# VectorE's order in the down stage as one chain, with a third of the bank reads as ScalarE copies and accumulating DMAs

## The chip, the cores and the metric

The kernel runs on one core of a Trainium2 chip. Its engines are TensorE (matmuls and transposes; PE, its weight loads PEld), VectorE (DVE), ScalarE (ACT) and GpSimd (POOL); SyncE (SP) issues most of the DMAs, POOL the rest. Each engine has its own queue of instructions, taken in order. The metric is the device time of one execution in microseconds (us), as the median of several runs.

## What is computed

A two-layer encoder step on 1024 prompt tokens and 8 x 16 sample tokens: 1152 rows of 1024 features, nine tiles of 128 rows. Each layer is attention (sliding window with sinks in layer 0, chunked attention over a shared K/V in layer 1) and a squared-ReLU MLP. Only the second half of the MLP and its neighbours matter here:

```python
def mlp(x, g_norm, w_up, w_down):
    return jnp.square(jax.nn.relu(rmsnorm(x, g_norm) @ w_up)) @ w_down

for layer in range(DEPTH):          # DEPTH = 2
    ...                             # attention, residual added to hp and hs
    hp = hp + mlp(hp, g_mlp[layer], w_up[layer], w_down[layer])
    hs = hs + mlp(hs, g_mlp[layer], w_up[layer], w_down[layer])
```

Everything is float32. A float32 product is made of three matmuls on operands split into a high part (rounded, made by ScalarE as a cast) and a low part (the rest, made by VectorE as a subtraction): high x high, high x low, low x high. In the code that is `split` (lines 125 to 134) and `mm3` (line 744).

## The kernel before

The stages of a layer follow each other: `attention`, `wo_phase`, `mlp_up`, `mlp_down`. Instructions are written in the order of the program, and a scheduler then fixes each engine's order by a simulated timeline, with priorities and with added order edges (`behind`, line 750, puts one instruction behind another on its engine). The order on the chip is static.

**The up stage** (line 778) computes h = relu(x w_up)^2 in 16 blocks of 256 features. After each pair of blocks, `forms_even` and `forms_odd` (lines 917 and 929) build, with VectorE, sums and differences of h between token groups, and store 20 such forms to DRAM (`hd`, through POOL's queue, 192 KB a store).

**The down stage** (line 967) is h w_down plus the residual, by a fast matrix multiplication: 20 products (`RANK`) per half of the hidden features, two halves, so 40 products per layer. The nine token tiles are three parts of three (`PARTS`: part 0 is tiles 5, 6, 7; part 1 is 2, 3, 4; part 2 is the sample tile, 0 and 1), the columns two halves of 512, so there are six outputs `o`; `o // 2` is the part. One product takes a form of h (`a`, 128 x 1536 floats, one for all three tiles of a part) and a sum or difference of blocks of w_down (`w`, 128 x 2048), and multiplies in three blocks, one per tile: 3 x 4 x 3 = 36 matmuls of 512 columns into three PSUM banks. The products stand in chains (`CHAINS`): within a chain the banks go on accumulating, and after a product the banks may be read and added to, or subtracted from, outputs. The chains and signs give 41 reads per layer, each of three banks (line 1115: VectorE, 128x512, `x = x + or - bank`), so 123 instructions.

Around product n, in program order:
- `load_w(n + 3)` loads the blocks of w_down that are not there yet (tiles `r`, 1 MB each), `load_h` the next form (768 KB, tile `a`); `a` has three buffers, chosen by `slot`, but only two for the last six products (`TAIL`). All these loads and those of the residual tiles `x` run on SP's queue in one chain (`load`, line 1026).
- `split_w(n + 1)` makes the high and low part of w and of a for the next product: two ScalarE casts, two VectorE subtractions. w has two buffers.
- `add_w(n + 2)` sums two blocks of w_down on VectorE into `s` (two buffers); eight of the 40 products use one block alone and need no sum, and the last four sum in place in `r`.
- the matmuls of the three blocks, each followed by its reads.

All nine residual tiles `x` (512 KB each) are loaded early: parts 2 and 1 before product 0, part 0 around product 2 (`X_AT`, keyed by n + `AHEAD`). When a part has had its last read it is stored: to `xd` in DRAM for the next layer, or to the output.

`DOWN_HOME` (line 1773) lists the down stage's tiles in the order of their addresses; a tile can be loaded once the up stage's tile at the same address is no longer used. `RAW_AT` says which `r` buffer takes which block of w_down. The last `forms_odd` of the up stage is written at a lowered priority (`LATER`), so VectorE does its sums during the first products of the down stage.

Of the kernel before, what the change touches and what calls it, by code (L numbers as in the profile page):

```python
# [8 lines left out]
F32 = mybir.dt.float32  # L9
# [40 lines left out]
NEG_H = ((4, 6), (6, 12, 1))  # L50
RAW_AT = ((1, 3, 2, 7, 0, 6, 9, 8), (5, 3, 10, 6, 7, 8, 4, 9))
EPS = 1e-6
# [42 lines left out]
class Build:  # L95
# [682 lines left out]
    def mlp_up(self, layer, sx, x8, rp, raw0):  # L778
        nc = self.nc
        tt = nc.vector.tensor_tensor  # L780
        with ExitStack() as st:
# [114 lines left out]
            for b in range(NFB):  # L896
                quad, ws = weights(b)
                eh = [hp.tile([P, 3 * 3 * P], F32, tag="h", name="h", bufs=7) for _ in range(2)]
                if b == 0:
                    tokens(eh, quad, ws, slice(0, 256), False)  # L900
                    tokens(eh, quad, ws, slice(256, 512), True)
                else:
                    tokens(eh, quad, ws, slice(0, 512), True)
                if b % 2 == 0:
                    even = eh
                    self.forms_even(b // 2, eh)
                else:
                    with self.tc.high_priority(-LATER) if b == NFB - 1 else nullcontext():
                        self.forms_odd(b // 2, even + eh, hp.tile([P, 3 * 3 * P], F32, tag="h", name="ht", bufs=7))

# [18 lines left out]
    def forms_odd(self, c, eh, extra):  # L929
        tt, put = self.nc.vector.tensor_tensor, self.form_store(c)  # L930
        add, sub = ALU.add, ALU.subtract
        (a0, s10, a8), (a1, a5, s11), (a2, a6, a10), (a3, a7, a11) = map(self.form_cut, eh)
        u, w, z = self.form_cut(extra)
# [33 lines left out]
    def mlp_down(self, layer, out):  # L967
# [3 lines left out]
        with ExitStack() as st:  # L971
            self.psum_pools(st, f"dn{layer}", dict(z=(2, 1), c=(6, 1)), dict(c="c"))
            kinds = dict(
                a=([P, 2, 4, 3 * P], F32R), w=([P, 2, 4, 512], F32R), r=([P, 4, 512], F32),
                s=([P, 4, 512], F32), x=([P, D], F32),
            )
            homes, slots, xs = {}, {}, {}
# [8 lines left out]
            for n, tags in enumerate(DOWN_HOME):  # L986
                pool = self.pool(st, f"d{n}_{layer}")
                for t in tags.split():
# [5 lines left out]
                    else:  # L994
                        homes[t] = pool
                        slots[t] = fresh(t)
            for t in range(NTILE):
                xs[t] = slots.pop(f"x{t}")

            N = [slice(0, 512), slice(512, 1024)]  # L1000
# [22 lines left out]
            def slot(n):  # L1023
                return 1 + n % 2 if n >= total - TAIL else n % 3

# [21 lines left out]
            def add_w(n):  # L1047
# [13 lines left out]
                if g < 0:  # L1061
                    x, y = y, x
                tt(src[n], x, y, ALU.add if plus else ALU.subtract)  # L1063

            def split_w(n):
                if n >= total:
                    return
                w = ws[n] = take(f"w{n % 2}")
                self.split(w[:, 0], w[:, 1], src.pop(n))
                a = aa[n]  # L1070
                self.split(a[:, 0], a[:, 1], a[:, 1].bitcast(F32))

            banks = None

            def early(n):
                return self.tc.high_priority(EARLY[n]) if n < len(EARLY) else nullcontext()

            def load_x(i):
                for t in PARTS[i]:
                    load(xs[t], self.xd[t])  # L1080

            for n in range(AHEAD):
                with early(n):
                    load_w(n)
                    load_h(n)
                if n in X_AT:
                    load_x(X_AT[n])
            add_w(0)
            split_w(0)
            add_w(1)  # L1090
            for n, (s, p, g, first, final, reads, _) in enumerate(seq):
                if layer == 0 and n == RANK:
                    self.prep_bias(self.dp)
                if n + AHEAD < total:
                    load_w(n + AHEAD)
                if n + AHEAD in X_AT:
                    load_x(X_AT[n + AHEAD])
                split_w(n + 1)
                add_w(n + 2)
                if first:  # L1100
                    banks = [self.psum("c", [P, 512], "ps_c") for _ in range(3)]
                a, w = aa.pop(n), ws.pop(n)
                for i in range(3):
                    c = slice(i * P, i * P + P)
                    z = [
# [6 lines left out]
                    self.follow(z[0][0], z[-1][1])  # L1112
                    for o, v in reads:
                        x = xs[PARTS[o // 2][i]][:, N[o % 2]]
                        tt(x, x, banks[i], ALU.add if v > 0 else ALU.subtract)  # L1115
                    for part in {o // 2 for o, _ in reads}:
                        if last[part] == n:
                            t = PARTS[part][i]
                            nc.sync.dma_start(out(t), xs[t])
                for m in range(n + 1, total):  # L1120
                    if m not in aa:
# [65 lines left out]
    def run(self):  # L1187
# [9 lines left out]
        with ExitStack() as top:  # L1197
# [556 lines left out]
def make_plan(tail, second):  # L1754
# [78 lines left out]
```

## Time and profile before

| | us |
|---|---|
| median of 3 runs | 2372.1 (2372.06 to 2375.68) |
| profiled execution, device time | 2365.98 |
| its span, first to last instruction | 2364.2 |
| down stage of layer 0, first matmul to the next stage's first | 802.7 to 1146.1 |
| down stage of layer 1, first matmul to the last one's end | 2021.7 to 2359.8 |
| TensorE's mean granted clock | 0.995 |

In a group's row stand the line, the engine, the operation, the tiles (out<-in, buffer numbers left out), the shape and the count; then busy us and mean ns of one; then the idle time of the engine just before these instructions, and what ended it. In a timeline row stand start and length in us, and in brackets the idle time before and its releaser. Since matmuls are pipelined, the bar of one (0.39 us) overlaps the next; the pace is the distance between starts. A row "SPq" or "POOLq" of the DMA list ends in the median us from issue to landing.

### The profile page before, as it was taken

How to read it: one execution, taken by the hardware profiler on the slowest of the kernel's cores; microseconds unless marked ns; L12 is line 12 of the kernel's file. 1: busy time of each engine (PE TensorE's matmuls, PEld its weight loads, DVE VectorE, ACT ScalarE, POOL GpSimd, SP SyncE). 2: the span in 40 equal slices, each digit the busy share in tenths (PEclk: the TensorE clock that was granted, in tenths of full speed). 3: DMA queues.
4: the chain of work that ended last, by engine and by line, in shares of the span. 5: the costliest groups of instructions: out<-in, count | busy, mean ns of one | idle time of the engine just before them, and what ended most of it. 6: DMA issues, size and time to landing. Idle time of an engine off the chain costs nothing.

```text
span 2364.2 us, 33257 instructions
## 1 busy us (share of the span) xinstructions
PE 2276.7 (96%) x11429; PEld 1891.4 (80%) x11429; DVE 1783.0 (75%) x3192; ACT 1274.2 (54%) x2503; POOL 574.4 (24%) x892
## 2 busy tenths in 40 slices
PE   7998999899999999999999999998999999999999
PEld 6787877788888778777878788887888888788777
DVE  6788786766656699998577876877665665998995
ACT  3777675555555444434277666665655555443432
POOL 4334332313213100001233434454122222100000
PEclk9999999999999999999999999999999999999999
DMA  7335546234434762635543655555243443835433
GB/s 252 124 113 165 173 141 208 94 119 160 137 112 152 285 231 96 216 113 199 174 153 113 200 164 170 168 172 172 88 148 126 137 146 125 328 120 182 148 120 107
DMA packets 216377, 375.38 MB, mean 159 GB/s; under 512 B 51144, under 2 KB 125840, under 8 KB 216208
## 3 DMA queue, kind: packets, MB, share of 16 engines
q1 hardware_dynamic: 193136, 300.89, 38.9%
q0 software_dynamic: 21776, 67.65, 7.8%
q10 hardware_dynamic: 1296, 4.72, 0.5%
q8 instruction: 90, 1.47, 0.3%
q14 instruction: 79, 0.65, 0.1%
HBM read 241.23 MB, written 130.90 MB: 157 GB/s over the span
## 4 chain that ended last, share of the span: by engine, by line
PE 66%; DVE 14%; DMA 11%; ACT 4%; issue 3%; POOL 1%; SPq 1%; DVEq 0%; ACTq 0%; POOLq 0%
PE ps_c L748 5%; PE ps_x L746 5%; PE ps_c L746 5%; PE ps_c L747 5%; PE ps_x L748 5%; PE ps_x L747 5%; PE ps_mm L217 3%; DMA r<-in_w_down 3%; PE ps_mm L219 3%; PE ps_mm L218 3%; DVE w L134 2%; PE ps_y L748 2%; PE ps_y L747 2%; PE ps_y L746 2%; PE ps_tr L324 2%
## 5 line engine op out<-in xcount | busy, mean ns | idle before, releaser
L746 PE MATMUL ps_c<-w,a 128*128 128x512 f32 x960 | 376.1, 392 | 9.1 <-DVE x L1115 8.2
L747 PE MATMUL ps_c<-w,a 128*128 128x512 f32 x960 | 375.5, 391 | 6.0 <-DVE w L134 5.9
L748 PE MATMUL ps_c<-w,a 128*128 128x512 f32 x960 | 374.9, 391 | 3.3 <-DVE a L134 3.2
L912 POOL DMA_DIRECT2D hd<-h x272 | 147.8, 544 | 592.1 <-ACT h L820 370.5
L746 PEld LDWEIGHTS ps_c<-w,a 128*128 128x128 f32 x960 | 180.6, 188 | 53.4 <-issue 5.1
L128 ACT CAST a<-a 128x1536 fp32r<-128x1536 f32 x80 | 118.9, 1486 | 190.4 <-DMA a<-hd 190.4
L747 PEld LDWEIGHTS ps_c<-w,a 128*128 128x128 f32 x960 | 180.6, 188 | 46.6 <-DVE w L134 9.9
L748 PEld LDWEIGHTS ps_c<-w,a 128*128 128x128 f32 x960 | 180.6, 188 | 42.3 <-DVE a L134 5.1
L128 ACT CAST w<-s 128x2048 fp32r<-128x2048 f32 x56 | 107.3, 1916 | 148.5 <-PE ps_c L748 134.9
L217 PE MATMUL ps_mm<-w,hh 128*128 128x512 f32 x432 | 172.8, 401 | 7.5 <-POOL w L185 3.1
L1115 DVE TENSOR_TENSOR x<-x,ps_c 128x512 f32<-128x512 f32 x246 | 160.5, 685 | 19.1 <-PE ps_c L748 19.1
L219 PE MATMUL ps_mm<-w,hl 128*128 128x512 f32 x432 | 172.0, 399 | 0.9 <-DMA hl<-hTd 0.8
L218 PE MATMUL ps_mm<-w,hh 128*128 128x512 f32 x432 | 171.1, 397 | 1.5 <-DVE w L190 1.3
L134 DVE TENSOR_TENSOR a<-a 128x1536 fp32r<-128x1536 f32 x80 | 140.4, 1756 | 39.6 <-ACT a L128 37.7
L746 PE MATMUL ps_x<-sx,w 128*128 128x512 f32 (+1 forms) x408 | 157.8, 387 | 3.7 <-ACT h L867 2.7
L128 ACT CAST w<-ru 128x512 fp32r<-128x512 f32 (+1 forms) x160 | 110.2, 708 | 83.7 <-PE ps_y L747 32.0
L748 PE MATMUL ps_x<-sx,w 128*128 128x512 f32 (+1 forms) x408 | 154.1, 378 | 0.0
L747 PE MATMUL ps_x<-sx,w 128*128 128x512 f32 (+1 forms) x408 | 154.1, 378 | 0.0
L134 DVE TENSOR_TENSOR ptl<-ps_tr,pth 128x512 fp32r<-128x512 f32 x180 | 122.6, 686 | 24.2 <-ACT pth L128 18.4
L1063 DVE TENSOR_TENSOR s<-r,r 128x2048 f32<-128x2048 f32 x56 | 128.1, 2289 | 13.3 <-DMA r<-in_w_down 13.3
L134 DVE TENSOR_TENSOR w<-ru,w 128x512 fp32r<-128x512 f32 (+1 forms) x160 | 126.9, 795 | 14.8 <-ACT w L128 14.7
L134 DVE TENSOR_TENSOR w<-s,w 128x2048 fp32r<-128x2048 f32 x56 | 128.2, 2289 | 4.1 <-ACT w L128 3.9
(277 smaller groups left out, 5896.8 us busy)
## 6 DMA issues: line engine op xcount, KB each, us to landing
a<-hd SPq DMA_DIRECT2D x80, 768.0 KB, 4.3
hd<-h POOLq DMA_DIRECT2D x272, 192.0 KB, 2.5
ru<-in_w_up SPq DMA_DIRECT2D x64, 512.0 KB, 3.8
r<-in_w_down SPq DMA_DIRECT2D x32, 1024.0 KB, 9.8
x<-xd SPq DMA_DIRECT2D x41, 512.0 KB, 6.8
o<-oTd SPq DMA_DIRECT2D x52, 256.0 KB, 5.1
xd<-xo SPq DMA_DIRECT2D x18, 512.0 KB, 2.8
xo<-xd SPq DMA_DIRECT2D x18, 512.0 KB, 3.7
```

The source lines that it names most:

```text
L128: a = nc.scalar.copy(hi, src)
L134: return a, e.tensor_tensor(lo, src, hi.bitcast(F32), ALU.subtract)
L217: nc.tensor.matmul(ps, a, w[:, 0, k, :], start=(k == 0), stop=False)
L218: nc.tensor.matmul(ps, a, w[:, 1, k, :], start=False, stop=False)
L219: self.lp = nc.tensor.matmul(ps, b, w[:, 0, k, :], start=False, stop=(k == KC - 1))
L324: self.lp = nc.tensor.transpose(pt[:, i, :], get(i), self.ident)
L746: a = mm(ps, ah, bh, start=first, stop=False, skip_group_check=True)
L747: mm(ps, ah, bl, start=False, stop=False, skip_group_check=True)
L748: return a, mm(ps, al, bh, start=False, stop=last, skip_group_check=True)
L912: return lambda p, z: self.nc.gpsimd.dma_start(self.hd[c // 4][:, p, c % 4], z)
L1063: tt(src[n], x, y, ALU.add if plus else ALU.subtract)
L1115: tt(x, x, banks[i], ALU.add if v > 0 else ALU.subtract)
```

## The change

Five things change in the down stage, and two beside it.

1. VectorE's order is written as one chain of order edges (`chain`): for product n the low parts of a and of w for n + 1, the reads of blocks 0 and 1, the sum for n + 2, the reads of block 2, then up to three of the sums of the last `forms_odd` (`self.late`; the lowered priority goes, `LATER` becomes that count of 3). `split_w` is divided into `split_h` and `split_w`.
2. A read whose part of `x` is not loaded yet becomes three ScalarE copies (with the sign as a scale) into a tile `o` (128 x 3 x 512, two buffers) and one DMA from POOL's queue that adds it to the residual in DRAM. With the new `X_AT` these are the reads after products 0, 1, 2, 3, 4, 8, 9, 10, 11, 12, 14, 28, 31 and 32.
3. The `x` tiles are loaded from POOL's queue, after product 1 (part 2), 12 (part 1) and 32 (part 0). Their first reads on VectorE follow after products 5, 15 and 37.
4. `a` keeps three buffers to the end, except that the last product takes buffer 1.
5. `RAW_AT` and `DOWN_HOME` are new: nine `r` buffers instead of eleven; `o0` and `o1` and the `s` tiles stand where `s0`, `s1`, `r0`, `r1`, `r2` stood.
6. The residual in DRAM is three tensors, one per part, instead of nine.
7. Every `forms_odd` collects its sums in `self.late`; only those of the last one are put in the chain.

```diff
-RAW_AT = ((1, 3, 2, 7, 0, 6, 9, 8), (5, 3, 10, 6, 7, 8, 4, 9))
+RAW_AT = ((7, 8, 9, 10, 0, 6, 4, 3), (3, 9, 5, 4, 8, 6, 10, 7))
...
-                    with self.tc.high_priority(-LATER) if b == NFB - 1 else nullcontext():
-                        self.forms_odd(b // 2, even + eh, hp.tile([P, 3 * 3 * P], F32, tag="h", name="ht", bufs=7))
+                    self.forms_odd(b // 2, even + eh, hp.tile([P, 3 * 3 * P], F32, tag="h", name="ht", bufs=7))
...
+        self.late = []
+        tt = lambda *z: self.late.append(self.nc.vector.tensor_tensor(*z))
...
             def slot(n):
-                return 1 + n % 2 if n >= total - TAIL else n % 3
+                return 1 if n == total - 1 else n % 3
...
             def load_x(i):
                 for t in PARTS[i]:
-                    load(xs[t], self.xd[t])
+                    xs[t] = take(f"x{t}")
+                    nc.gpsimd.dma_start(xs[t], self.xd[t])
...
             add_w(0)
+            split_h(0)
             split_w(0)
             add_w(1)
+            self.dve = None
+
+            def chain(z):
+                if self.dve is not None:
+                    self.behind(self.dve, z)
+                self.dve = z
+                return z
+
+            for z in (*low[0], total_of.get(1)):
+                if z is not None:
+                    chain(z)
+            late = iter(self.late)
             for n, (s, p, g, first, final, reads, _) in enumerate(seq):
...
-                if n + AHEAD in X_AT:
-                    load_x(X_AT[n + AHEAD])
+                split_h(n + 1)
                 split_w(n + 1)
                 add_w(n + 2)
+                for z in low.get(n + 1, ()):
+                    chain(z)
...
+                adds = {}
+                for o, v in reads:
+                    if PARTS[o // 2][0] not in xs:
+                        adds[o] = take(f"o{no % 2}")
+                        no += 1
                 for i in range(3):
+                    if i == 2 and n + 2 in total_of:
+                        chain(total_of[n + 2])
...
                     for o, v in reads:
+                        if o in adds:
+                            nc.scalar.activation(adds[o][:, i], banks[i], AF.Copy, scale=float(v))
+                            continue
                         x = xs[PARTS[o // 2][i]][:, N[o % 2]]
-                        tt(x, x, banks[i], ALU.add if v > 0 else ALU.subtract)
+                        chain(tt(x, x, banks[i], ALU.add if v > 0 else ALU.subtract))
...
+                for o, z in adds.items():
+                    dst = self.xp[o // 2][:, :, N[o % 2]].rearrange("t p n -> p t n")
+                    nc.gpsimd.dma_start(dst, z, accum_op=ALU.add)
+                if n in X_AT:
+                    load_x(X_AT[n])
+                for _, z in zip(range(LATER), late):
+                    chain(z)
...
-            self.xd = [dram([P, D], f"xd{t}") for t in range(NTILE)]
+            self.xp = [dram([3, P, D], f"xp{i}") for i in range(3)]
+            self.xd = {t: self.xp[i][n] for i in range(3) for n, t in enumerate(PARTS[i])}
...
 DOWN_HOME = (
-    "s0", "s1", "r0", "r1", "r2", "r3", "x5", "x6", "x7", "bias", "r4", "r5", "+384", "x8", "x0", "x2", "+640",
+    "s1", "r0", "o0", "+512", "s0", "o1", "+512", "r3", "x5", "x6", "x7", "bias", "r4", "r5", "+384", "x8", "x0", "x2", "+640",
     "a0", "x1", "x3", "x4", "r6", "a1", "a2", "w0", "w1", "r7", "r8", "r9", "r10",
 )
 TAIL = 6
-LATER = 400
+LATER = 3
 AHEAD = 3
-X_AT = {0: 2, 1: 1, 5: 0}
+X_AT = {1: 2, 12: 1, 32: 0}
```

More of the change, by code (lines that the diff above doesn't have):

```diff
@@ L929, in forms_odd @@
     def forms_odd(self, c, eh, extra):
-        tt, put = self.nc.vector.tensor_tensor, self.form_store(c)
+        put = self.form_store(c)
         add, sub = ALU.add, ALU.subtract
+        self.late = []
+        tt = lambda *z: self.late.append(self.nc.vector.tensor_tensor(*z))
         (a0, s10, a8), (a1, a5, s11), (a2, a6, a10), (a3, a7, a11) = map(self.form_cut, eh)
@@ L975, in mlp_down @@
                 s=([P, 4, 512], F32), x=([P, D], F32),
+                o=([P, 3, 512], F32),
             )
@@ L996, in mlp_down @@
                         slots[t] = fresh(t)
-            for t in range(NTILE):
-                xs[t] = slots.pop(f"x{t}")
             N = [slice(0, 512), slice(512, 1024)]
@@ L1062, in add_w, with split_h @@
                     x, y = y, x
-                tt(src[n], x, y, ALU.add if plus else ALU.subtract)
+                total_of[n] = tt(src[n], x, y, ALU.add if plus else ALU.subtract)
             def split_w(n):
[L1066 to L1071, printed above, removed]
+                if n < total:
+                    w = ws[n] = take(f"w{n % 2}")
+                    low[n].append(self.split(w[:, 0], w[:, 1], src.pop(n))[1])
+            def split_h(n):
+                if n < total:
+                    a = aa[n]
+                    low[n] = [self.split(a[:, 0], a[:, 1], a[:, 1].bitcast(F32))[1]]
+            low, total_of = {}, {}
             banks = None
+            no = 0
             def early(n):
@@ L1085, in mlp_down @@
                     load_h(n)
-                if n in X_AT:
-                    load_x(X_AT[n])
             add_w(0)
+            split_h(0)
             split_w(0)
             add_w(1)
+            self.dve = None
[8 more added lines that the diff above has]
+            late = iter(self.late)
             for n, (s, p, g, first, final, reads, _) in enumerate(seq):
```

## The prediction

> **What bounds the kernel now.** I read the page's busy shares first, then stage windows restricted to the matmuls of the down stage (`ps_c`), then the groups of one down stage, and last the timelines around TensorE's stalls.
>
> ```profile
> span 2364.2 us, 33257 instructions
> PE 2276.7 (96%) x11429; PEld 1891.4 (80%) x11429; DVE 1783.0 (75%) x3192; ACT 1274.2 (54%) x2503; POOL 574.4 (24%) x892
> ```
>
> TensorE is the bound on average, so only time in which it waits, or runs slowly, can be won. Three windows of the down stage (the columns are length, then busy time and count by engine, granted clock, DMA share, GB/s):
>
> ```profile
> 2097.20:2187.00 89.80, 89.80 (x398) 74.35 (x396) 20.73 (x32) 1.00 0.48 167
> 802.70:1146.10 343.40, 332.88 (x1440) 269.70 (x1439) 79.48 (x122) 1.00 0.53 182
> 2021.70:2359.80 338.10, 330.08 (x1440) 268.89 (x1439) 79.69 (x122) 1.00 0.45 159
> ```
>
> The first is products 9 to 19 of the second layer: no wait, 11 products x 36 matmuls = 396 (two more only touch the edges). That gives 89.8 / 11 = 8.163 us per product, and 40 products would take 326.5 us. The two down stages take 343.4 and 338.1 us. The surplus is 16.9 + 11.6 = **28.5 us**, all that the down stages hold for any reordering. (The idle time in the groups below is smaller, since a matmul's 390 ns bar overlaps the next one's.)
>
> Who causes it? The second layer's down stage by groups:
>
> ```profile
> L746 PE MATMUL ps_c<-w,a 128*128 128x512 f32 x480 | 187.6, 391 | 4.0 <-DVE x L1115 4.0
> L747 PE MATMUL ps_c<-w,a 128*128 128x512 f32 x480 | 187.4, 390 | 2.9 <-DVE w L134 2.9
> L748 PE MATMUL ps_c<-w,a 128*128 128x512 f32 x480 | 186.9, 389 | 1.1 <-DVE a L134 1.1
> ...
> L1115 DVE TENSOR_TENSOR x<-x,ps_c 128x512 f32<-128x512 f32 x123 | 80.4, 686 | 11.4 <-PE ps_c L748 11.3
> L134 DVE TENSOR_TENSOR a<-a 128x1536 fp32r<-128x1536 f32 x39 | 68.5, 1757 | 9.1 <-ACT a L128 9.0
> L134 DVE TENSOR_TENSOR w<-s,w 128x2048 fp32r<-128x2048 f32 x28 | 64.1, 2290 | 4.0 <-ACT w L128 3.9
> L1063 DVE TENSOR_TENSOR s<-r,r 128x2048 f32<-128x2048 f32 x27 | 61.7, 2290 | 6.9 <-DMA r<-in_w_down 6.8
> L128 ACT CAST a<-a 128x1536 fp32r<-128x1536 f32 x39 | 58.0, 1486 | 91.1 <-DMA a<-hd 91.1
> L128 ACT CAST w<-s 128x2048 fp32r<-128x2048 f32 x28 | 53.7, 1917 | 72.9 <-PE ps_c L748 63.6 <-DVE s L1063 4.0 <-DVE a L134 2.7
> L134 DVE TENSOR_TENSOR w<-r,w 128x2048 fp32r<-128x2048 f32 x11 | 25.2, 2292 | 4.3 <-ACT w L128 4.3
> ```
>
> Every wait of TensorE ends with VectorE. VectorE's rows add to 80.4 + 68.5 + 64.1 + 61.7 + 25.2 = 300 us of 338, four sums written in place not counted: a second bound just behind the first, so the order of its work decides. This is how it goes wrong:
>
> ```profile
> 2247.56 1.29 DVE L1115 TENSOR_TENSOR x<-x,ps_c 128x512 f32<-128x512 f32 x2
> 2248.76 1.76 DVE L134 TENSOR_TENSOR a<-a 128x1536 fp32r<-128x1536 f32 x1
> 2250.43 2.48 DVE L1115 TENSOR_TENSOR x<-x,ps_c 128x512 f32<-128x512 f32 x4
> 2252.82 2.29 DVE L1063 TENSOR_TENSOR s<-r,r 128x2048 f32<-128x2048 f32 x1
> 2255.02 2.29 DVE L134 TENSOR_TENSOR w<-s,w 128x2048 fp32r<-128x2048 f32 x1
> 2257.22 0.69 DVE L1115 TENSOR_TENSOR x<-x,ps_c 128x512 f32<-128x512 f32 x1
> ```
> ```profile
> 2258.06 0.47 PE L746 MATMUL ps_c<-w,a 128*128 128x512 f32 x1 [2.12 <-DVE x L1115]
> ```
>
> The read at 2257.22 is of a bank that TensorE had filled some 7 us earlier (product 27 began at 2247.5, a block takes a third of 8.16 us); a sum and a split ran ahead of it, and TensorE stands 2.12 us for that bank. The starts also give VectorE's cost back to back: 2.20 us for a 128x2048 sum or split, 1.67 for the a split, 0.60 for a read.
>
> In the first layer the seam between the two w_down halves shows a sum waiting for its weights with a split queued behind it, and the tail shows waits for the single a buffer ahead:
>
> ```profile
> 967.78 2.29 DVE L1063 TENSOR_TENSOR s<-r,r 128x2048 f32<-128x2048 f32 x1 [3.69 <-DMA r<-in_w_down]
> ```
> ```profile
> 1110.34 0.50 PE L746 MATMUL ps_c<-w,a 128*128 128x512 f32 x1 [0.67 <-ACT a L128]
> ...
> 1112.18 0.50 PE L748 MATMUL ps_c<-w,a 128*128 128x512 f32 x1 [1.11 <-DVE a L134]
> ```
> ```profile
> 1112.00:1116.00 4.00, 3.82 (x10) 3.08 (x11) 3.49 (x5) 1.23 (x3) 1.27 (x2) 0.60 0.96 358
> ```
>
> Right after those two waits the granted clock is 0.60 for 4 us: 10 matmuls instead of 17 or 18, about 1.7 us lost besides the waits.
>
> **The change part by part.** *The chain.* Per product VectorE now does: a split of the next product (1.67), w split of the next (2.20), reads of blocks 0 and 1, the sum for the product after next (2.20, absent where one weight block is used alone), reads of block 2. A product with one read per block costs 6.07 + 1.8 = 7.9 us, with two 9.7, against 8.16. Take the hard place, products 29 and 30 with two reads each. ScalarE's w cast ends some 2.5 us into a product, so w ends at 4.7; block-0 reads end at 5.9, block-1 reads at 7.1; the sum, where there is one, at 9.3; block-2 reads 1.2 later. VectorE leaves a product with two reads and a sum about 2.3 us behind TensorE. A second such product, 1.5 us over, makes it about 3.8; 29 and 30 do not both have a sum (31 uses one block alone), so about 2.9 is reached. TensorE waits when the lag exceeds 8.16 - 3.87 - 1.2 = 3.1 us (block 0 must be read before the next product reuses it) or 4.3 (w split); 3.87 is the a and w splits together, 1.2 two reads. So the fixed order just holds, with 0.2 us to spare at one place and 0.8 or more elsewhere, and the down stage's waits for VectorE fall to about nothing. The row at 967.78 keeps its late weights, but now the split of product 20 goes ahead of that sum, so TensorE doesn't see it.
>
> *Reads moved to ScalarE.* 14 x 3 = 42 reads of 0.60 leave VectorE per layer (25 us). The nearest row for their copies:
>
> ```profile
> L227 ACT COPY qr<-ps_mm 128x512 f32<-128x512 f32 x36 | 21.1, 586 | 0.0
> ```
>
> 42 x 0.59 = 25 us go to ScalarE. Beside the a cast and the w cast of a product (1.49 and 1.92 by the groups above) that makes 3.4 + 1.8 = 5.2 of 8.16. The last copy delays the next w cast by 0.6, inside the 2.5 used above. By itself this part is worth little on top of the chain: it is slack.
>
> *Accumulating DMAs.* 14 per layer, 768 KB each, issued on POOL, which has nothing else there but the last stores of `hd`. No row shows one. Bounds on issue to landing:
>
> ```profile
> a<-hd SPq DMA_DIRECT2D x80, 768.0 KB, 4.3
> ...
> r<-in_w_down SPq DMA_DIRECT2D x32, 1024.0 KB, 9.8
> x<-xd SPq DMA_DIRECT2D x41, 512.0 KB, 6.8
> ...
> xd<-xo POOLq DMA_DIRECT2D x9, 512.0 KB, 3.1
> ```
>
> Below, the POOL stores: 3.1 us for 512 KB, about 4 for 768. Above, twice the slowest load row, 20 us, because the target is read as well. I take 7 us, near the stores, whose direction and queue it shares. Two places ask for it. Each of the two `o` buffers is refilled two products later, so a landing under 8.16 + 2.72 - 0.6 = 10.3 us is hidden, and another 4.8 us is hidden by the bank's own slack. Product 15 reads x part 1, whose load waits for the accumulation of product 12: 2 x 8.16 + 2.72 = 19.0 us less 0.6 for the copy, 6.8 for the load and 1.6 allowed for issuing three leaves **10.0 us**. Seven fits both. Cost 0; without that cover it is the slower rival below.
>
> *x loads.* They leave SP, where they held what came after:
>
> ```profile
> 820.03 8.47 SPq L1027 DMA_DIRECT2D x<-xd x3
> 828.62 0.36 SPq L1027 DMA_DIRECT2D a<-hd  x1
> ```
> ```profile
> 802.70:819.40 16.70, 16.65 (x74) 13.44 (x73) 16.70 (x22) 7.40 (x7) 6.24 (x12) 1.00 1.03 407
> ```
>
> The a load stood 8.5 us behind x tiles whose memory was still in use. At the start the DMA engines are full (share 1.03), and 4.7 MB of x leave that stretch while five accumulations (3.9 MB, read and written) enter the first 41 us. I take 2 us per layer for loads late there; bounds 0 and 5 (this layer's waits in products 3 to 8 of today).
>
> *Seam and tail.* Where the up stage ends, a read of `ps_y` sits behind the first down splits:
>
> ```profile
> 799.88 0.50 PE L746 MATMUL ps_y<-sx,w 128*128 128x512 f32 x1 [1.73 <-DVE h L878]
> ```
>
> With x out of the way those splits come earlier; the scheduler sets that order, so I take 1 us gained of a possible 3 for two layers. The 16 late forms (384 columns each, so shorter than a read of 512) fall three per product into products 0 to 5, which have no reads on VectorE until 5. In the tail, a keeps three buffers until product 38; only product 39's load comes one product ahead. A load of 4.3, the cast and the split make 1.49 + 1.67 + 4.3 = 7.5 of 8.16 us, and that load row is a median: I charge 0.5.
>
> Sum: 326.5 + 2 + 0.5 + 0.5 for small hiccups = 329.5, say 330 per layer. Gain 13.4 + 8.1 + 1 = **22 us**. The profiled execution is 2364.2 of span, 2366.0 in all, 6.1 below the shown median of 2372.1; taking 22 off both gives 2344 and **2350**.
>
> By the Trainium skill, "TensorE: Matmul & The Clock Gate", section "Part 1: The HAM clock gate", the clock falls after an idle window of about 3.4 us. The windows' 0.60 followed only 1.8 us of idle time, so the measurement doesn't fit the rule's plain reading; by the rule the 1.7 us would not be tied to these waits and could stay, and the sum would be 2352.
>
> **The rivals.** *Order gives half back.* The margin of 0.2 to 0.8 us at products with two reads doesn't hold, because a cast or load comes a microsecond late, and the strict order then holds everything behind it. About ten such products a layer at 0.5 us each: 10 us back, 2360. For it: the thin margin. Against: moved reads lower the lag before each.
>
> *No change.* The stalls only move, into the attention that follows or the seam, since a static order is rebuilt everywhere. 2372. Against: TensorE runs without a break from one stage into the next today, with VectorE lightly loaded at the tail.
>
> *Accumulations land late.* One mechanism: landing beyond 10 us makes product 15's reads late, beyond 15.1 it also holds ScalarE's copies and so banks. Price per layer at 18 us: 8 less 2 of slack at product 15, and 2.9 at each of four products (2, 4, 10, 12; the others gain from the delay before them) = 17.6, twice 35, less 22 gained: 13 slower, **2385**. It decides from about 16.7 us, where 2 x (4.7 + 4 x 1.6) = 22. For it: the first products' full DMA. Against: every POOL row lands within 3.1.
>
> In the Trainium skill, "Collectives: The Full Stack", section "The bandwidth ceiling: the fold count and why AG ≠ RS ≠ AR", an add inside a transfer runs at half a copy's rate because it reads two sources. No trace here shows it; as an estimate that would double the 4 us of a plain store to 8, which still fits.
>
> **How the numbers follow.** Forecast 0.54 (own range 2343 to 2358), half back 0.20, no change 0.09, late accumulations 0.17. A measurement of this kernel tells about 0.2%, 4.7 us, from no change. Faster: 0.54 + 0.20 = 0.74; same 0.09; slower 0.17. Low end: all 28.5 + 3 us won, 2340. The high end takes in no change and the late case up to about 17.3 us of landing, 2378.
>
> **What would show it.** Right: both down stages at 327 to 333 us, TensorE's idle time there under 4 us per layer, no wait of VectorE for x at product 15, accumulations landing in 4 to 10 us, no slow clock near product 36. Wrong: TensorE waiting for ScalarE's copies in products 2 to 4 or 10 to 12, POOL idle for landings longer than 10 us, DVE idle at product 15 for a DMA into x, or down stages still near 340 with waits for other splits.

## The result, and the profile after

The changed kernel takes **2400.85 us** (median of 4 runs, 2398.5 to 2405.0) where the kernel before takes 2373.1 in the same session: ratio 1.0117, 95% interval 1.0100 to 1.0135. It is slower by 1.2%, outside the predicted range of 2340 to 2378. The profiled execution has a span of 2403.2 us, 39.0 more than before. The medians differ by 27.8: the execution profiled here lies 4 us above its kernel's median, the one before 6 to 7 below its own, so some 11 of the 39 us lie between single executions.

The head of its page, and then the windows of the two down stages, cut to the `ps_c` operations as before (length; PE, PEld, DVE and ACT busy; granted clock, DMA share, GB/s); the third window is products 8 to 18 of the second layer:

```profile
span 2403.2 us, 33331 instructions
PE 2285.3 (95%) x11429; PEld 1904.2 (79%) x11429; DVE 1735.2 (72%) x3108; ACT 1317.3 (55%) x2587; POOL 632.8 (26%) x938
```
```profile
810.05:1168.19 358.14, 332.86 (x1440) 272.99 (x1439) 51.40 (x80) 24.48 (x42) 0.97 0.72 208
2055.43:2398.69 343.26, 329.59 (x1440) 271.78 (x1439) 51.66 (x80) 24.82 (x42) 0.98 0.66 190
2135.00:2225.00 90.00, 90.00 (x398) 74.55 (x398) 9.55 (x15) 10.72 (x18) 1.00 0.80 211
```

The windows divide the 39 us. The first down stage starts 7.3 us later than before (810.05 against 802.7) and takes 14.7 more; from its end to the start of the second it takes 11.6 more; the second takes 5.2 more. Past its first products the second layer's stage runs as forecast: 90.0 us busy of 90.0 at products 8 to 18. The loss sits in a few places. The second down stage by groups (busy, mean ns, idle before and what ended it):

```profile
L746 PE MATMUL ps_c<-w,a 128*128 128x512 f32 x480 | 188.1, 392 | 12.5 <-ACT o L1138 12.5
L747 PE MATMUL ps_c<-w,a 128*128 128x512 f32 x480 | 187.7, 391 | 1.2 <-DVE w L134 1.2
L748 PE MATMUL ps_c<-w,a 128*128 128x512 f32 x480 | 187.5, 391 | 0.0
...
L1141 DVE TENSOR_TENSOR x<-x,ps_c 128x512 f32<-128x512 f32 x81 | 52.3, 682 | 14.5 <-PE ps_c L748 12.2 <-ACT o L1138 2.2
...
L1138 ACT ACTIVATE o<-ps_c 128x512 f32<-128x512 f32 x42 | 24.8, 596 | 41.7 <-DMA xp<-o 25.0 <-PE ps_c L748 16.6
...
L1148 POOL DMA_DIRECT2D xp<-o x14 | 18.2, 1300 | 226.9 <-ACT o L1138 176.0 <-issue 33.7 <-DMA xp<-o 17.1
```

Before, every wait of TensorE here ended with VectorE. Now TensorE has one long wait, for ScalarE's copies into `o`; the copies wait 25.0 us for accumulations to land, and GpSimd stands 33.7 us before accumulations with nothing shown that it waits for (`issue`). The timelines of that place, products 0 to 4 of the second layer, GpSimd first, then ScalarE's copies and TensorE:

```profile
2065.17 1.36 POOL L1148 DMA_DIRECT2D xp<-o  x1 [5.83 <-ACT o L1138]
2076.98 1.28 POOL L1148 DMA_DIRECT2D xp<-o  x1 [10.44 <-issue]
2077.79 1.06 POOL L911 DMA_DIRECT2D hd<-h  x1
2084.81 0.58 POOL L911 DMA_DIRECT2D hd<-h  x1 [5.96 <-issue]
2085.70 1.61 POOL L1084 DMA_DIRECT2D x<-xp  x3 [0.31 <-issue]
2087.30 1.09 POOL L911 DMA_DIRECT2D hd<-h  x2
2096.88 1.32 POOL L1148 DMA_DIRECT2D xp<-o  x1 [8.49 <-issue]
...
2079.66 1.30 ACT L1138 ACTIVATE o<-ps_c 128x512 f32<-128x512 f32 x2
2108.49 1.08 ACT L1138 ACTIVATE o<-ps_c 128x512 f32<-128x512 f32 x2 [17.49 <-DMA xp<-o]
...
2109.14 0.79 PE L746 MATMUL ps_c<-w,a 128*128 128x512 f32 x1 [12.51 <-ACT o L1138]
```

Product 2's copies end at 2079.66 + 1.30 = 2080.96. Their accumulation is issued at 2096.88, 15.9 us later, behind the accumulation of product 1, the three loads of x part 2 and stores of `hd`. Product 4's copies, which need the same buffer, start at 2108.49, when it has landed, 11.5 after the issue. The first layer has the same wait: product 5 starts 13.95 us late there, 12.7 here. The granted clock then falls:

```profile
2109.00:2117.00 8.00, 7.86 (x25) 6.33 (x26) 0.68 (x1) 1.19 (x3) 0.70 0.79 147
```

Product 5 takes 10.5 us instead of 8.16 (9.8 in the first layer). Product 4's wait and product 5's clock come to 12.7 + 2.3 and 13.95 + 1.6, **30.5 us** in two layers. Other places of the first layer: 8.5 us at products 9 to 11 (a late a load, the bias transfers, one more wait for `o`), 4.8 at 35 and 36; product 39 costs 4.0 in the two layers together. At product 35 VectorE works on the next layer's weights, which are not in the chain, ahead of the split for product 36:

```profile
1124.89 3.38 DVE L190 SCALAR_TENSOR_TENSOR w<-raw,gcol,w 128x512 fp32r<-128x512 f32 x3 [2.50 <-POOL w L185]
1128.19 2.28 DVE L134 TENSOR_TENSOR w<-r,w 128x2048 fp32r<-128x2048 f32 x1
```

TensorE then waits 3.14 us for a read. The order edges hold the chain's own instructions in order and keep no others out. Together the places named, 47.8 us, are nearly all of the 48.4 that the down stages take beyond 2 x 326.5.

The seam, where the forecast had a small gain, is a loss:

```profile
802.67 2.29 DVE L1062 TENSOR_TENSOR s<-r,r 128x2048 f32<-128x2048 f32 x1
804.87 0.68 DVE L878 TENSOR_TENSOR h<-ps_y,h 128x512 f32<-128x512 f32 x1
...
805.61 0.50 PE L746 MATMUL ps_y<-sx,w 128*128 128x512 f32 x1 [3.92 <-DVE h L878]
```

The sum for product 1 now also stands ahead of the read of `ps_y`: 3.92 us of wait, and 3.60 in the second layer, against 1.73 and 1.12 before. Between the middle of the up stage and the first product the two layers lose 4.2 and 4.9 us against before: 4.7 of wait, the rest the slower clock after it.

### The profile page after: what moved, and what is told of

Same layout as the page of the kernel before. It is cut to its first block, busy times and chain, and to the rows that moved or that the text cites. A ratio compares the mean times of both kernels' runs of the same rounds, so it can differ in the third digit from the quotient of the medians.

```text
span 2403.2 us, 33331 instructions
## 1 busy us (share of the span) xinstructions
PE 2285.3 (95%) x11429; PEld 1904.2 (79%) x11429; DVE 1735.2 (72%) x3108; ACT 1317.3 (55%) x2587; POOL 632.8 (26%) x938
## 3 DMA queue, kind: packets, MB, share of 16 engines
q0 software_dynamic: 35568, 99.11, 14.5%
## 4 chain that ended last, share of the span: by engine, by line
PE 76%; DVE 8%; DMA 7%; issue 4%; ACT 3%; POOL 1%; SPq 0%; ACTq 0%; POOLq 0%; DVEq 0%
PE ps_c L746 7%; PE ps_c L747 7%; PE ps_c L748 7%; PE ps_x L746 5%; PE ps_x L748 5%; PE ps_x L747 5%; PE ps_mm L217 4%; PE ps_mm L219 3%; PE ps_mm L218 3%; PE ps_y L746 2%; PE ps_y L748 2%; PE ps_y L747 2%; DMA a<-hd 2%; PE ps_tr L324 2%; PE ps_mm L176 1%
## 5 line engine op out<-in xcount | busy, mean ns | idle before, releaser
L746 PE MATMUL ps_c<-w,a 128*128 128x512 f32 x960 | 377.5, 393 | 36.0 <-ACT o L1138 27.8
L1148 POOL DMA_DIRECT2D xp<-o x28 | 36.3, 1297 | 464.2 <-ACT o L1138 364.6
L128 ACT CAST pth<-ps_tr 128x512 fp32r<-128x512 f32 x180 | 105.0, 595 | 45.7 <-PE ps_tr L324 37.2
```

The lines of the kernel that those rows point to most:

```text
L128: a = nc.scalar.copy(hi, src)
L746: a = mm(ps, ah, bh, start=first, stop=False, skip_group_check=True)
L1148: nc.gpsimd.dma_start(dst, z, accum_op=ALU.add)
```

## The experiments

All ratios are to the kernel before, run on the same chip in the same session. "Late at product 4" is how much later than its usual pace TensorE starts product 5 because of `o`, first and second layer, from the traces. Waits given below without a row are such delays too; since a matmul's bar overlaps the next, they are about 0.16 us longer than the idle time in a row.

| kernel | us | ratio (95%) | down stages, us | late at product 4 |
|---|---|---|---|---|
| the change | 2400.85 | 1.0117 (1.0100 to 1.0135) | 358.1, 343.3 | 13.95, 12.7 |
| e1_plain | 2374.19 | 1.0017 (1.0002 to 1.0031) | 343.1, 332.9 | 0.95, 3.1 |
| e2_ring | 2396.32 | 1.0096 (1.0070 to 1.0122) | 350.2, 334.8 | 4.8, 4.2 |
| e3_chain_alone | 2369.99 | 0.9989 (0.9975 to 1.0004) | 349.2, 332.9 | none |
| e4_no_chain | 2413.76 | 1.0181 (1.0155 to 1.0207) | 370.1, 347.1 | 16.7, 3.3 |
| e5_ring96 | 2393.05 | 1.0102 (1.0065 to 1.0139) | 350.7, 340.0 | 4.9, 9.8 |
| e6_seam | 2394.23 | 1.0093 (1.0076 to 1.0110) | 357.7, 343.9 | 13.3, 12.8 |
| e7_x2_early | 2369.32 | 0.9991 (0.9980 to 1.0002) | 352.0, 328.0 | none |
| e8_few | 2358.98 | 0.9949 (0.9934 to 0.9964) | 340.9, 329.7 | none |
| e9_x2_later | 2401.29 | 1.0146 (1.0108 to 1.0184) | 356.6, 345.2 | 3.5, 3.8 |
| e10_one | **2354.97** | 0.9935 (0.9920 to 0.9950) | 336.5, 329.5 | none |
| e11_tail | 2361.07 | 0.9956 (0.9941 to 0.9971) | 341.0, 328.0 | none |
| e12_best | 2360.89 | 0.9957 (0.9942 to 0.9972) | 344.9, 328.0 | none |

**Plain stores in place of the accumulations.** The order on every engine is the same; the stores overwrite the residual instead of adding to it.

```diff
-                    nc.gpsimd.dma_start(dst, z, accum_op=ALU.add)
+                    nc.gpsimd.dma_start(dst, z)
```

> The 28 DMAs that add to the residual in DRAM become plain stores to the same place (the sums of these reads with the residual are left out); every engine's order is the same. Theory R (room on POOL's queue): an adding DMA takes about twice the descriptors of a store, and the queue has room for one such DMA and little else, so the next large DMA starts only when the one before has landed. A plain store of 768 KB then leaves room for a second one: the second store starts within 1.5 us of its last copy (now 5.6 us later), the waits for ScalarE's copies at the end of product 4 (14.0 and 12.7 us) fall under 3 us each, total 2372 to 2382. Theory T (the transfer itself is slow and the DMA engines are full): the landing falls from 7.7 to about 4.5 us, the waits shrink by some 3 us per transfer but the stores still start late, total 2385 to 2395.

Of the 1.17% lost, 1.00 goes with one argument. The DMA queue and the issues of these transfers, the changed kernel first (packets, MB, share of 16 engines; then count, size, median us to landing), then this run:

```profile
q0 software_dynamic: 35568, 99.11, 14.5%
...
xp<-o POOLq DMA_DIRECT2D x28, 768.0 KB, 7.7
```
```profile
q0 software_dynamic: 30192, 99.11, 11.2%
...
xp<-o POOLq DMA_DIRECT2D x28, 768.0 KB, 5.2
```

With the same bytes, an accumulation takes (14.5% of 2403 us - 11.2% of 2372 us) / 28 = 3.0 us more of all 16 DMA engines than a plain store, and lands 2.5 us later at the median. So the adding is what costs, not the copies. It doesn't yet say how 2.5 us become 13: the time is what the room theory forecast, but the run takes away both the transfer time and, by that theory, the room, so it can't decide between the two.

**More room for transfer descriptors on GpSimd's queue.** First 1920 bytes per partition, then 1536. Both take it from gaps in the address list; the order on every engine stays that of the change, but for one store that ScalarE issues in the run with 1920.

```diff
-    nc = bacc.Bacc("TRN2", ..., dynamic_dma_scratch_size=1024)
+    nc = bacc.Bacc("TRN2", ..., dynamic_dma_scratch_size=1536)
```

> The changed kernel with 1920 bytes per partition of descriptor memory for POOL's queue in place of 1024 (one gap in the down stage's address list and the pad at the end pay for it). The DMAs still add. Theory R: two adding DMAs fit at a time, so the third one (product 2) starts within 2 us of its last copy (now 20 us later), the waits at the end of product 4 fall under 3 us each, total 2370 to 2382. Theory T: the adding DMAs land as slowly as now or slower, as they overlap; the waits stay above 8 us each and the total above 2390.

> The changed kernel with 1536 instead of 1024 bytes per partition for GpSimd's transfer descriptors; the order of instructions on every engine is the same, so only the room differs. Room theory (at 1024 bytes one accumulation leaves too little room for anything else of size, so transfers on GpSimd's queue go one at a time): the waits of ScalarE's copies for o at the end of product 4 (13.95 and 12.67 us) fall by more than half, because hd stores and x loads may now stand beside an accumulation, and the time falls by 8 to 16 us to 2385 to 2393; the five accumulations in products 8 to 12, issued 7.8 us apart after each landing, stay one at a time, since two of them still don't fit. Transfer theory (each accumulation takes the 16 DMA engines for about 7 us whatever the room): the waits at product 4 stay above 9 us and the time within 5 us of 2401.

With 1920 bytes the second accumulation of the first layer is issued 8.3 us after the first, which takes 12.1 to land: two stand side by side. The lateness at product 4 is 4.8 and 4.2 us, between the two forecasts (under 3, above 8), and the time, 2396, is the transfer theory's. GpSimd's timeline with 1536 bytes, first layer:

```profile
830.80 1.29 POOL L1148 DMA_DIRECT2D xp<-o  x1 [10.58 <-issue]
831.60 1.65 POOL L911 DMA_DIRECT2D hd<-h  x2
838.85 1.61 POOL L1084 DMA_DIRECT2D x<-xp  x3 [5.61 <-DMA xp<-o]
840.51 1.09 POOL L911 DMA_DIRECT2D hd<-h  x2
841.60 1.35 POOL L1148 DMA_DIRECT2D xp<-o  x1
854.70 1.33 POOL L1148 DMA_DIRECT2D xp<-o  x1 [7.41 <-issue]
```

Product 2's accumulation is now issued right behind the x loads (841.60); in the change GpSimd stands idle for 9.9 us at that point. But it takes 12.8 us to land instead of 8.8 (in the second layer 16.5 instead of 11.5), beside loads that are still under way. The wait falls from 13.95 to 4.9 in the first layer and from 12.7 to 9.8 in the second. So the room is part of the wait, and the transfers themselves are the rest; neither theory holds alone. As a time the gain isn't resolved: the intervals of e2, e5 and the change overlap.

**x part 2 off GpSimd's queue.** It is loaded by SP before product 0, so products 0 and 1 read on VectorE and 12 accumulations a layer are left.

```diff
+                    if i in (2,):
+                        load(xs[t], self.xd[t])
+                    else:
+                        nc.gpsimd.dma_start(xs[t], self.xd[t])
...
-X_AT = {1: 2, 12: 1, 32: 0}
+X_AT = {12: 1, 32: 0}
```

> The changed kernel with x part 2 loaded by SP before product 0, as in the kernel before; so products 0 and 1 read on VectorE, 12 reads a layer stay accumulations, and no x load stands on GpSimd's queue until product 12. Theory that the queue is too full in products 0 to 4 (five large transfers, three x loads and the hd stores, one at a time): the wait of ScalarE's copies at product 4 falls from 13 us to under 3 us in both layers and the time falls by about 20 us, to 2375 to 2382. Theory that accumulations are slow wherever they stand: products 2, 3, 4 and again 8 to 12 wait for o by 3 us or more and the time stays above 2390.

The second layer's down stage:

```profile
2030.53:2358.55 328.02, 326.86 (x1440) 270.01 (x1439) 55.57 (x86) 21.30 (x36) 1.00 0.66 195
```

328.0 us for 40 products, 1.5 above the pace of 326.5, with 12 accumulations, three of them at products 2 to 4 and five at 8 to 12: no wait for `o`. Accumulations that the queue has time for cost nothing there. The time falls further than the 20 us forecast, to 2369.3; the first down stage starts earlier too (802.4 against 810.1). The first layer's stage still takes 352.0: it loses about 18 us at products 7 to 11, where its bias transfers run (7.0 us for an x read at product 7, 2.4 for another at product 9 and for `o` at 11, and the clock after them).

**x part 2 loaded later**, after product 6, so that no x load stands among the first accumulations (16 a layer, seven in a row).

```diff
-X_AT = {1: 2, 12: 1, 32: 0}
+X_AT = {6: 2, 12: 1, 32: 0}
```

> The changed kernel with x part 2 loaded after product 6 instead of product 1: products 5 and 6 become accumulations too (16 reads a layer), and products 0 to 6 put seven of them on GpSimd's queue with no x load among them. Theory that the queue's length is what counts (an accumulation about 7.8 us, the first 11.5, the x loads about 10 together, hd stores 2 us or less each): without the x loads the wait at product 4 falls from 13 us to under 3, and at products 5 or 6 up to 5 us may be left, since seven accumulations and the hd stores need about all the time; 2380 to 2392. Theory that accumulations of themselves hold up the copies: with two more of them the waits for o come to 13 us or more again and the time is 2400 or more.

Both forecasts were half right. Product 4's lateness falls to 3.5 and 3.8 us, so about 9 to 10 of the 13 were the x loads ahead. But the total didn't move: the second layer waits again at products 6, 9, 10 and 12 (2.6, 1.6, 1.3 and 1.8 us, the second of them for an x read, the others for `o`) and its stage takes 345.2; the first loses 11.8 us at products 9 and 10, against 6.7 in the change. The queue has two accumulations more to carry, and the lateness comes in smaller pieces, with a slow clock at products 5 and 7 (0.76 and 0.83).

**The chain alone**, no accumulation, and **the change without the chain**. In the first, parts 2 and 1 are loaded by SP before product 0, part 0 after product 2 (for which six late forms a product make room), and all reads are VectorE's; in the second, the edges between VectorE's instructions are gone.

```diff
-X_AT = {1: 2, 12: 1, 32: 0}
+X_AT = {2: 0}
-LATER = 3
+LATER = 6
```
```diff
             def chain(z):
-                if self.dve is not None:
-                    self.behind(self.dve, z)
-                self.dve = z
                 return z
```

> The chain without any adding DMA: all x tiles are there before their first read (parts 2 and 1 on SP's queue before product 0 as before the change, part 0 on POOL's queue after product 2), all 41 reads are VectorE's, six late forms per product in place of three. Theory C (the chain is what helps, the moved reads are slack): no wait for ScalarE's copies, both down stages at 327 to 333 us, total 2350 to 2362 unless the seam before product 0 stays as late as in the changed kernel (then 2358 to 2368). Rival: without the moved reads VectorE has no room and the fixed order makes waits of 1 us and more at products with two reads, both down stages at 335 to 345 us.

> The changed kernel with its adding DMAs and its late x loads, but no order edges for VectorE. Theory C: the waits for ScalarE's copies at product 4 stay (12 to 14 us each) and waits for VectorE come back in products 12 to 39 (now none in layer 1), 4 to 8 us per layer; total 2405 to 2418. Rival (the moved reads alone free VectorE, the chain is idle): products 12 to 39 stay without waits, total 2398 to 2404.

Without the chain the change takes 13 us more, and the old waits are back (in the second layer 2.3 us for an x read at the end of product 27, 1.3 for w at 20 and 21); products 20 to 30 lose 8.2 and 5.8 us in the two layers, where the change loses nothing. With the chain and no accumulation the second layer's stage takes 332.9, although the six late forms hurt it:

```profile
2049.17 1.49 DVE L932 TENSOR_TENSOR h<-h 128x384 f32<-128x384 f32 x3
2050.69 1.03 DVE L932 TENSOR_TENSOR ht<-ht,h 128x384 f32<-128x384 f32 x2
2051.64 0.55 DVE L932 TENSOR_TENSOR h<-h 128x384 f32<-128x384 f32 x1
2052.11 1.75 DVE L134 TENSOR_TENSOR a<-a 128x1536 fp32r<-128x1536 f32 x1
```

They stand 2.9 us ahead of the next split, and TensorE starts product 3 exactly 2.9 us late in both layers. A strict order makes every instruction put into it a charge on all behind it. The forecast of 2350 to 2362 was missed, at 2370.0, no different from the kernel before: the first layer's stage takes 349.2. Its bias transfers run at products 3 to 7 there; the a load issued at 847.02 among them takes 17.8 us to land, and products 6 to 8 lose 12.6. The chain with no accumulation and three late forms was not run.

**The seam.** The sum for product 1 goes behind the read of `ps_y`.

```diff
-                b = tt(v[3], Y, v[3], ALU.add)
+                b = self.seam = tt(v[3], Y, v[3], ALU.add)
...
             add_w(1)
+            self.behind(self.seam, total_of[1])
```

> The changed kernel with VectorE's sum for product 1's weights put behind the up stage's last-but-one read of ps_y (L878). Theory that the sum ahead of that read makes the seam's waits of 3.93 and 3.60 us: both fall to 1.1 to 1.7 us, the time falls by 4 to 5 us, to about 2396. Theory that the order written out moves other work into the seam anyway: the waits stay above 3 us and the time within 2 us of 2401.

The wait is back to 1.7 us in both layers (before the change 1.73 and 1.12):

```profile
802.21 0.50 PE L746 MATMUL ps_y<-sx,w 128*128 128x512 f32 x1 [1.73 <-DVE h L878]
...
2043.83 0.50 PE L746 MATMUL ps_y<-sx,w 128*128 128x512 f32 x1 [1.72 <-DVE h L878]
```

The first down stage starts at 805.08 instead of 810.05, and the kernel takes 6.6 us less than the change, somewhat more than expected, with intervals that overlap. By the rows, the sum's place was the cause of the wait.

**Few accumulations.** Parts 2 and 1 by SP before product 0, as above; part 0 after product 14 (four accumulations a layer, at products 4, 8, 10, 14), then after product 4 (one).

```diff
-X_AT = {1: 2, 12: 1, 32: 0}
+X_AT = {14: 0}
```
```diff
-X_AT = {14: 0}
+X_AT = {4: 0}
```

> x parts 2 and 1 loaded by SP before product 0, part 0 by GpSimd after product 14; only 4 reads a layer (products 4, 8, 10, 14) stay copies with accumulations, two products or more apart, the other 37 reads are VectorE's in the same chain, three late forms per product as in the changed kernel. Theory that accumulations cost nothing where the queue has time for them, and that the chain alone removes the old stalls: no wait for o anywhere, the second layer's down stage 327 to 331 us, the first layer's 332 to 345 (its bias transfers come beside products 6 to 9), the seams 1.7 us or less as in the run of the chain alone; 2358 to 2366. Theory that an accumulation costs wherever it is: 2370 or more.

> As the run with 4 accumulations a layer, but x part 0 loaded after product 4, so only product 4's read stays an accumulation. Theory that spaced accumulations cost nothing: within 3 us of the 2359 of that run, unless the earlier x load meets the first layer's bias transfers (then up to 5 us more). Theory that each costs about 1 us: 2355 to 2357.

Both are faster than the kernel before, by 0.5% and **0.65%**. Their second down stages, four and then one:

```profile
2022.82:2352.51 329.69, 327.14 (x1440) 270.01 (x1439) 71.17 (x110) 7.12 (x12) 1.00 0.53 173
```
```profile
2019.19:2348.64 329.45, 327.13 (x1440) 269.93 (x1439) 77.14 (x119) 1.78 (x3) 1.00 0.49 167
```

They differ by 0.2 us, so three more spaced accumulations cost nothing in the second layer. In the first the stage falls from 340.9 to 336.5: beside the bias transfers, accumulations at products 8 and 10 took 13.8 and 11.4 us to land, and the waits at product 11 that follow (0.5 us for `o`, 1.95 for an x read) are gone with them. The forecast of 1 us for each accumulation gave the time, but the stages say otherwise. The times' intervals overlap; which of the two is the faster isn't settled by them.

**The tail and the bias.** On top of four accumulations, product 39 alone has w's split ahead of a's; then also w's first split goes behind L878, and the bias transfers behind product 22's a load.

```diff
-                for z in low.get(n + 1, ()):
+                for z in low.get(n + 1, ())[:: -1 if n + 2 == total else 1]:
                     chain(z)
```
```diff
+            self.behind(self.seam, low[0][1])
...
-            nc.sync.dma_start(tb, self.ins["rel_bias_b"][0])
+            self.behind(sp, nc.sync.dma_start(tb, self.ins["rel_bias_b"][0]))
```

> The run with 4 accumulations a layer, with the chain's order turned round for product 39 alone: w's split before a's, whose load comes one product ahead. Theory that w's split stands behind the late a there: the waits of 1.56 and 2.1 us before product 39's second matmul (for w) go or become a wait for a of 0.5 us or less in the second layer; 1 to 3 us less than that run, 2356 to 2358. Theory that w's own cast is late: the wait stays.

> The run with product 39 turned round, plus two edits: w's first split of the down stage goes behind the up stage's last-but-one read of ps_y (L878), and the first layer's bias transfers go behind product 22's a load on SP's queue instead of beside products 6 to 9. If the seam's wait of 1.73 us in the first layer and the waits of 1.88 to 1.95 us at products 9 and 11 come from these: both go, 2350 to 2355. If the bias transfers only meet other loads later: no gain or a loss of up to 5 us, 2356 to 2364.

The first takes product 39's wait away in the second layer (329.7 to 328.0), not in the first, where the wait for w stays and one of 1.3 us for a comes after it: there w's cast is late, not its place in the order. The time doesn't show it. The second clears the seam's waits and products 9 and 11, and product 22 ends 5.6 us late instead, with a slow clock behind: the bias transfers cost at both places where these runs put them, beside loads. Neither is worth keeping on these times.

## Why the prediction was wrong

**The bound and the chain: right in the second layer.** There the waits for VectorE that were to go are gone, and the lag stayed within its limit: products 6 to 38 run at 8.16 us. The forecast of 330 us per stage is what the second layer takes once the queue is relieved (329.5 and 329.7). The first takes 336.5 at best, with 1.4 us lost at products 2 and 3, 2.1 at 8 and 9 beside the bias transfers, 4.1 at 35 to 38 and 2.3 at 39, where the sum had 2 for x loads and 1 for the tail and small hiccups. The best run gains 15.9 us on the kernel before in its session, of the 22 forecast.

**Moved reads: right that they are slack, and no more than that.** With all but one of them back on VectorE the kernel is the fastest. The copies also bring a dependence that was not priced: a copy that waits for `o` stands in ScalarE's queue, and the casts of the next products behind it (at product 4 the next cast starts at 2109.47, right behind the copies that waited 17.49).

**Accumulating DMAs, "Cost 0": the step that failed.** The time from issue to landing was put at 7 us, and it is 7.2 to 7.8 where nothing disturbs it. I tested it against the room of one buffer (10.3 us, with the bank's slack 15.1) and took the queue as free: "nothing else there but the last stores of `hd`". That left out two things. The same change put three x loads on that queue after product 1. And at 1024 bytes of room an accumulation lets nothing of its size, nor x loads with stores, stand beside it, so the queue carries these one after the other, accumulations 7.7 us apart at best. What counts is copy to landing: 15.9 us of waiting for its turn and 11.5 for landing, 27.4 against 15.1; the 12.3 over are nearly all of TensorE's 12.5. The sum to make was that of the queue. From the first issue to the third landing it carries three accumulations, three x loads and the stores, 2108.39 - 2065.17 = 43.2 us, while TensorE wants the bank that product 4's copies are to empty from 2096.5 on, 31 us after that first issue. Removing the adding (e1), the x loads ahead (e9, e7) or some of the room limit (e5) each removes the wait or a part of it.

The Trainium skill, "DMA: Bandwidth & Descriptors", section "SWDGE vs HWDGE vs iDMA", says that descriptors of transfers issued by GpSimd are written to rings in on-chip memory, one for the read and one for the write of each DMA operation. The rows agree in that more of this memory let an accumulation be issued earlier (841.60 against 855.26); how many descriptors one takes no run here counts.

**x loads, 2 us per layer: wrong.** Moved off SP's queue, they became 9 to 10 of the 13 us at product 4. They were charged to the queue they left and not to the one they joined.

**Seam, 1 us gained: wrong**, 4.7 us of wait and 4.4 of slow clock lost, by the sum for product 1, which the change puts ahead of the chain; the run of the seam shows it. **Tail, 0.5 per layer:** 1.6 and 2.4. The prediction had also named "no slow clock near product 36", and the clock there is 0.84 in the first layer. **Not in the sum:** 13.3 us at products 9 to 11, 35 and 36 of the first layer. At 9 and 10 e1, without the adding, loses 9.8 as well, and e10 only 1.8. And attention and up stages slower by 3.1 us in the first layer and 6.7 in the second. In the second layer the runs with one and four accumulations lose 6.7 and 3.3 there as well, so much of it isn't the transfers' doing; and at 9.8 together it is no more than the 11 us between single executions, so it isn't shown to be the change's at all.

**The rivals.** "Accumulations land late" came out on the right side with a price that was too small, 2385 against 2401, and with the wrong half of the mechanism: it asked how long one takes to land, 18 us at the price given. The longest in the change took 13.1, so that its price came nearest is luck. The profile's sign for it, GpSimd idle beside late copies, was the right thing to name.

## What to carry to other kernels

When a transfer replaces engine work, add up what its queue must carry in the busiest stretch, with everything else that the change sends there, before comparing one transfer's landing with one buffer's slack. Move loads away from a stretch in which a queue is already full, and keep the slow kind of transfer to the few places that need it: one of the fourteen was enough here. In an order written out by hand, look at what each added instruction stands in front of, in the stages before and after too, and at what stands outside the order and can still get in between.

## What the runs showed of the hardware

An accumulating transfer of 768 KB lands in 7.2 to 7.8 us where nothing disturbs it and in up to 13.1 beside loads in the change (16.5 in e5), a plain store in 5.2 at the median. At products 8 to 12 of the second layer, where each is issued 0.3 us after the one before has landed, they run 7.7 to 8.0 us apart:

```profile
2157.40 1.30 POOL L1148 DMA_DIRECT2D xp<-o  x1 [10.75 <-DMA xp<-o]
2165.07 1.27 POOL L1148 DMA_DIRECT2D xp<-o  x1 [6.38 <-DMA xp<-o]
2172.97 1.28 POOL L1148 DMA_DIRECT2D xp<-o  x1 [6.62 <-issue]
2180.95 1.26 POOL L1148 DMA_DIRECT2D xp<-o  x1 [6.70 <-issue]
```

And the DMA engines are nearly full while they move few bytes; two windows of the change, the first with x and weight loads, the second with accumulations and `a` loads:

```profile
2084.00:2096.00 12.00, 12.00 (x54) 9.95 (x53) 11.31 (x10) 4.86 (x5) 3.27 (x6) 1.00 1.01 395
2157.00:2180.00 23.00, 23.00 (x103) 19.03 (x102) 19.16 (x10) 15.03 (x15) 3.85 (x3) 1.00 0.89 183
```

A share of 1.01 goes with 395 GB/s in the one, 0.89 with 183 in the other. The half rate that the Trainium skill's page "Collectives: The Full Stack" gives for an add (section "The bandwidth ceiling: the fold count and why AG ≠ RS ≠ AR"), with its estimate of 8 us in the prediction, roughly agrees with these. The landing did not double: it went from 5.2 us for a plain store to 7.7.
